# A hybrid SSD and S5 encoder block on one core: masks by affine selects on POOL, rows by one DMA from ACT's queue, a recurrence of three operations a step

## The chip, the cores and the metric

The kernel runs on one core of a Trainium2 chip. The metric is the device time of one execution in microseconds (us). Before the change three runs took 2913.18, 2923.3 and 2929.7 us; their median, 2923.3 us, is the time before. The engines are PE (TensorE, matrix products), DVE (VectorE), ACT (ScalarE), POOL (GpSimd) and SP (SyncE, which here only issues DMAs). Each engine works through its own queue of instructions in order; a wait at the head of a queue holds everything behind it.

## The reference, cut to what matters

One layer of an encoder for 2048 tokens of width 1024, float32 throughout. Beside projections and a feed-forward part it has two mixers, and the change lies in these two.

```
# SSD, per direction, per chunk of 128 tokens; 16 heads in 4 groups, state 128
a_cs  = cumsum(dt * a)                                   # along the chunk
seg   = exp(where(tril, a_cs[q] - a_cs[s], -inf))        # 128 x 128 per head
y     = (C B^T * seg) @ (x * dt)  +  C @ prev * exp(a_cs)
state = B^T @ (x * dt * exp(a_cs[end] - a_cs))           # one per chunk, then a scan over chunks
# S5, per direction: 32 groups of 16 channels, 64 complex states each
h[t] = A * h[t-1] + B u[t]                               # complex, diagonal A
y[t] = Re(C h[t])
```

The backward direction is the same with time reversed: its mask is the upper triangle.

## The kernel before, in words

The program has three large parts in time. Up to about 330 us the input is normalised and the S5 tables are made. From about 330 to 1170 us the SSD mixer and the S5 recurrence and outputs run. From there on come the output projection and the feed-forward part, which the change doesn't touch.

The SSD mixer works in two rounds: first the second half of the sequence (half = 1, chunks 15 down to 8), then the first half (half = 0, chunks 7 down to 0). In a round, `group` handles one of four head groups: `conv_tile` four times (matrix products of the projection on PE, copies out of PSUM on ACT, four multiply-adds at L692 and a gate at L695 on DVE), and then eight calls of `ssd_unit`, one per chunk. So a round has 32 units; this text numbers them 0 to 31 in the order worked.

A unit loads `rw`, the cumulated decays of 4 heads for both directions, copied to all 128 partitions (two DMAs of 256 KB from SP, L747), and `eb` (L751). It adds the mask `msk` (0 or -1e30) to both halves of `rw` (L753): on DVE in the first round (chunk 8 and above), on POOL in the second. ACT takes eight exponentials (L764) into `Lt`. DVE adds the two directions (L766) and multiplies by the scores (L767); PE multiplies by x (L770) and by the state (L776). DVE weights x for the chunk's own state, once for each direction (L790); PE makes that state (L791); ACT copies the forward one out (L795) and SP stores it (L796). `rw` and `Lt` have two buffers each, so the rows of a unit can be loaded once the exponentials of the unit two before it are done.

The S5 recurrence (`recur`, L336 to L350) walks over 126 steps of 128 x 64 numbers on POOL, four operations a step: two products with `s5ar` and `s5ai`, their sum, and the addition to `s5V`. Each step needs the one before. Then POOL issues 16 DMAs that store the states (`store_states`, L356), which the S5 outputs of the second round read.

The order of the instructions on each engine is fixed when the program is built, by a scheduler that simulates it with estimated times (`schedule_with_timeline_sim`). The recurrence's steps get priorities that spread them over the groups of the first round (L350's caller, RS = 0.9).

Of the kernel before, what the change touches and what calls it, by code (L numbers as in the profile page):

```python
# [17 lines left out]
P = 128  # L18
# [17 lines left out]
def bcast(ap, axis, n):  # L36
    a = [list(d) for d in ap.ap]
    a.insert(axis, [0, n])
    return bass.AP(ap.tensor, ap.offset, a)
# [63 lines left out]
class S5:  # L103


    def __init__(self, nc, tc, ident, keep, ps, pp, dr, prm, ud, ys_d):
        self.nc, self.tc, self.ident = nc, tc, ident
        self.keep, self.ps, self.pp, self.dr = keep, ps, pp, dr
        self.prm, self.ud, self.ys_d = prm, ud, ys_d
        self.od = dr.tile([NG5, 2, 2, 64, 256], F32, name="s5od")  # L110
        self.xd = dr.tile([NK5, P, 1024], F32, name="s5xd")
        self.vd = dr.tile([NG5, 2, 2, 64, P], F32, name="s5vd")
        self.td = dr.tile([16, NG5, 31, 16], F32, name="s5td")
        self.ar = keep.tile([P, 2, 32], F32, name="s5ar")
        self.ai = keep.tile([P, 2, 32], F32, name="s5ai")
        self.gb = keep.tile([P, 2, NG5], F32, name="s5gb")
# [4 lines left out]
    def params(self, cst, sp):  # L121
# [48 lines left out]
        for d in range(2):  # L170
            rows = slice(64 * d, 64 * d + 64)
            for g in range(2):
                src = pw[64 * g:64 * g + 64, 16, :, 16 * d:16 * d + 16]
                dr_ = self.ar[rows].rearrange("p r (k g) -> p r k g", g=2)[:, :, :, g]
                di_ = self.ai[rows].rearrange("p r (k g) -> p r k g", g=2)[:, :, :, g]
                v.tensor_copy(dr_, bcast(src[:, 0], 1, 2))
                v.tensor_scalar(di_[:, 0], src[:, 1], -1.0, None, ALU.mult)
                v.tensor_copy(di_[:, 1], src[:, 1])
        den = sp.tile(sh, F32, name="s5den")
# [156 lines left out]
    def recur(self, vp, at_step):  # L336
        nc = self.nc
        V = self.V[:, :, :, :]
        t0 = vp.tile([P, 2, NG5], F32, name="s5r0")
        t1 = vp.tile([P, 2, NG5], F32, name="s5r1")  # L340
        rs = NG5 * P
        at = lambda j: view(V, j, [[rs, 2], [P, NG5]])
        sw = lambda j: view(V, rs + j, [[-rs, 2], [P, NG5]])
        v = nc.gpsimd
        for j in range(1, P - 1):
            with at_step(j):
                v.tensor_tensor(t0, at(j - 1), self.ar, ALU.mult)
                v.tensor_tensor(t1, sw(j - 1), self.ai, ALU.mult)
                v.tensor_tensor(t0, t0, t1, ALU.add)
                v.tensor_tensor(at(j), at(j), t0, ALU.add)  # L350

# [65 lines left out]
class Block:  # L417
# [308 lines left out]

    def masks(self, cst):
        nc = self.nc
        self.msk = cst.tile([P, 2, P], F32, name="msk")
        nc.gpsimd.memset(self.msk, 0.0)  # L730
        nc.gpsimd.affine_select(self.msk[:, 0], self.msk[:, 0], pattern=[[1, P]], compare_op=ALU.is_ge,
                                fill=-1e30, base=0, channel_multiplier=-1)
        nc.gpsimd.affine_select(self.msk[:, 1], self.msk[:, 1], pattern=[[-1, P]], compare_op=ALU.is_ge,
                                fill=-1e30, base=0, channel_multiplier=1)


    def rows_bc(self, src_d, ch, r0, n):
        s = src_d[ch, r0:r0 + n, :]
        return s.rearrange("r t -> (r t)").partition_broadcast(P)

    def ssd_unit(self, sp, pp, g, ch, sl):
# [3 lines left out]
        rw = sp.tile([P, 2, 4, P], F32, name="rw", bufs=2)  # L745
        for d in range(2):
            nc.sync.dma_start(rw[:, d].rearrange("p h q -> p (h q)"), self.rows_bc(self.acs_d, ch, 16 * d + 4 * g, 4))  # L747
        eb = sp.tile([P, 2, P], F32, name="eb", bufs=2)
# [3 lines left out]
        for d in range(2):  # L752
            (v if ch >= 8 else nc.gpsimd).tensor_tensor(rw[:, d], rw[:, d], bcast(self.msk[:, d], 1, 4), ALU.add)  # L753
        pt = pp.tile([P, 512], F32, name="ptb", tag="tb", bufs=2)
# [29 lines left out]
        xw = sp.tile([P, 2, 4, 64], F32, name="xw", bufs=2)  # L784
        st = pp.tile([P, 512], F32, name="pst", tag="st", bufs=1)
        for d in range(2):
            if (d == 0 and ch == 15) or (d == 1 and ch == 0):
                continue
            wv = bcast(self.tok[:, 1, ch % 4, ch // 4, 16 * d + 4 * g:16 * d + 4 * g + 4], 2, 64)
            v.tensor_tensor(xw[:, d], xb[:, 0:256].rearrange("p (h q) -> p h q", h=4), wv, ALU.mult)  # L790
            nc.tensor.matmul(st[:, 256 * d:256 * d + 256], xb[:, 256:384], xw[:, d].rearrange("p h q -> p (h q)"),  # L791
                             start=True, stop=True)
            if d == 0:
                sf = sp.tile([P, 256], F32, name="sf", bufs=2)
                nc.scalar.copy(sf, st[:, 0:256])  # L795
                nc.sync.dma_start(self.sf_d[ch][:, g], sf)  # L796
            elif ch == 15:
# [400 lines left out]
def hybrid_block_kernel(ctx: ExitStack, tc: tile.TileContext, *aps):  # L1198
# [9 lines left out]
    with ExitStack() as mix:  # L1208
# [46 lines left out]
        with pool(name="s5v", bufs=1) as vp, ExitStack() as xs:  # L1255
# [8 lines left out]
            xp = xs.enter_context(pool(name="s5xa", bufs=1))  # L1264
            b.masks(late)
            b.sb = late.tile([P, 4, 256], F32, name="sb")
# [104 lines left out]
```

## Time and profile before

| | |
|---|---|
| median of three runs | 2923.3 us |
| the profiled execution, device time | 2930.28 us |
| its span in the trace | 2928.5 us |
| PE busy | 2701.5 us (92%) |
| DVE busy | 2197.4 us (75%) |
| ACT busy | 1364.4 us (47%) |
| POOL busy | 653.9 us (22%) |

The profile is of one execution. A line of a view names an engine, a line of the kernel, the operation and the tiles (written <- read), with the shape; "idle before" is how long the engine stood still ahead of it, and the name behind the arrow is what ended the wait. Shares over the whole span hide that the engines' load differs by stage, so the rows below are cut by stretches: the first round of units lies in about 329 to 718 us, the second in about 718 to 1170 us.

### The profile page before, as it was taken

The page shows a single profiled execution, that of the slowest core. Times are in us where ns is not written, and L with a number is a line of the kernel's source. Part 1 is how long each engine was busy: PE and PEld are TensorE (multiplying, and loading weights), DVE is VectorE, ACT ScalarE, POOL GpSimd, SP SyncE. Part 2 cuts the span into 40 slices and gives each one's busy share as a digit, 9 for nine tenths or more (in the row PEclk, how much of TensorE's full clock was granted, in tenths as well). Part 3 has the DMA queues.
Part 4 walks back from the last instruction along what each step waited for, and adds up shares of the span by engine and source line. Part 5 has one row for each costly group of instructions (what it writes and reads, how often), then busy time and mean ns, then how long its engine had stood idle before and what let it go on. Part 6 is the DMA issues. An engine that isn't in the chain of part 4 may idle for free.

```text
span 2928.5 us, 37294 instructions
## 1 busy us (share of the span) xinstructions
PE 2701.5 (92%) x12952; PEld 2181.7 (74%) x12952; DVE 2197.4 (75%) x3255; ACT 1364.4 (47%) x2329; POOL 653.9 (22%) x1133
## 2 busy tenths in 40 slices
PE   6998899876999998899898999999999999999997
PEld 4666899765877886677776878787877777877776
DVE  5997688786786776677767777779887888656587
ACT  4542455444567665334235444446444445333254
POOL 0443499992233332111120000000000000000012
PEclk9999999988999999999998999999999999999999
DMA  4546633448455656957845234325444337456464
GB/s 129 173 133 198 168 114 121 112 128 227 134 175 162 188 163 204 252 170 201 252 141 187 79 108 137 107 77 193 149 136 130 121 131 243 160 204 194 150 233 158
DMA packets 507400, 471.55 MB, mean 161 GB/s; under 512 B 90364, under 2 KB 417356, under 8 KB 507212
## 3 DMA queue, kind: packets, MB, share of 16 engines
q1 hardware_dynamic: 504972, 463.99, 52.4%
q0 software_dynamic: 2240, 5.18, 0.7%
q8 instruction: 102, 1.67, 0.2%
q14 instruction: 86, 0.70, 0.1%
HBM read 324.37 MB, written 144.67 MB: 160 GB/s over the span
## 4 chain that ended last, share of the span: by engine, by line
PE 40%; DMA 8%; DVE 7%; issue 2%; ACT 2%; POOL 1%; SPq 0%; ACTq 0%; DVEq 0%; POOLq 0%
PE pA L1040 17%; PE pB L1040 9%; PE pD L1040 5%; PE p L444 3%; PE p L445 2%; PE p L446 2%; DMA ar<-act_d 2%; DVE ll L440 1%; DMA bs<-in_ffn_w_down_dram 1%; DMA wr<-in_ffn_w_up_dram 1%; DMA bs<-hop_d 1%; DMA wt_d<-bs 1%; PE po L846 1%; DVE tl L1027 1%; DMA tst<-in_ffn_w_down_dram 0%
## 5 line engine op out<-in xcount | busy, mean ns | idle before, releaser
L1040 PE MATMUL pA<-th,lh 128*128 128x512 f32 x1056 | 423.7, 402 | 28.3 <-ACT pc L1088 18.8
L1040 PE MATMUL pA<-tl,lh 128*128 128x512 f32 x1056 | 422.1, 400 | 4.2 <-DVE tl L1027 4.2
L1040 PE MATMUL pA<-th,ll 128*128 128x512 f32 x1056 | 420.5, 399 | 0.8 <-DVE ll L440 0.8
L444 PE MATMUL pmm<-hh,wh 128*128 128x512 f32 (+1 forms) x896 | 333.9, 373 | 3.7 <-DVE zt L706 2.4
L445 PE MATMUL pmm<-hl,wh 128*128 128x512 f32 (+1 forms) x896 | 332.7, 371 | 0.0
L446 PE MATMUL pmm<-hh,wl 128*128 128x512 f32 (+1 forms) x896 | 330.2, 369 | 0.0
L1040 PEld LDWEIGHTS pA<-th,lh 128*128 128x128 f32 x1056 | 200.6, 190 | 86.7 <-ACT pc L1088 27.4
L1040 PEld LDWEIGHTS pA<-tl,lh 128*128 128x128 f32 x1056 | 200.7, 190 | 54.2 <-DVE tl L1027 6.4
L1040 PEld LDWEIGHTS pA<-th,ll 128*128 128x128 f32 x1056 | 200.6, 190 | 50.3 <-DVE ll L440 1.6
L1040 PE MATMUL pB<-tl,lh 128*128 128x512 f32 x528 | 209.6, 397 | 1.8 <-DVE tl L1027 1.8
L1040 PE MATMUL pB<-th,lh 128*128 128x512 f32 x528 | 209.7, 397 | 1.8 <-ACT lh L439 1.6
L1040 PE MATMUL pB<-th,ll 128*128 128x512 f32 x528 | 209.2, 397 | 0.0
L1088 ACT COPY pc<-pA 128x512 f32<-128x512 f32 x204 | 116.0, 584 | 185.4 <-PE pA L1040 184.4
L444 PEld LDWEIGHTS pmm<-hh,wh 128*128 128x128 f32 x896 | 169.9, 190 | 30.2 <-issue 3.7
L445 PEld LDWEIGHTS pmm<-hl,wh 128*128 128x128 f32 x896 | 169.8, 190 | 22.6 <-issue 2.5
L764 ACT ACTIVATE Lt<-rw,tokS 128x128 f32<-128x128 f32 x512 | 157.4, 389 | 61.3 <-PE pyd L770 48.7
L446 PEld LDWEIGHTS pmm<-hh,wl 128*128 128x128 f32 x896 | 169.6, 189 | 21.3 <-issue 1.1
L692 DVE SCALAR_TENSOR_TENSOR xbc<-rb,cw,xbc 128x1024 f32<-128x1024 f32 x128 | 178.7, 1399 | 3.8 <-ACT xbc L690 2.8
L444 PE MATMUL p<-wo,yh 128*128 128x512 f32 x384 | 157.3, 410 | 22.2 <-ACT yh L439 21.3
L439 ACT CAST lh<-s 128x512 fp32r<-128x512 f32 (+3 forms) x136 | 109.1, 815 | 123.8 <-DVE s L1007 71.2
L440 DVE TENSOR_TENSOR ll<-s,lh 128x1024 fp32r<-128x1024 f32 (+3 forms) x136 | 126.3, 933 | 52.5 <-PE pA L1040 43.7
L445 PE MATMUL p<-wo,yh 128*128 128x512 f32 x384 | 155.6, 405 | 0.0
(421 smaller groups left out, 6139.0 us busy)
## 6 DMA issues: line engine op xcount, KB each, us to landing
wr<-in_ffn_w_up_dram SPq DMA_DIRECT2D x88, 512.0 KB
rw<-acs_d SPq DMA_DIRECT2D x128, 256.0 KB
wraw<-in_w_in_dram SPq DMA_DIRECT2D x52, 512.0 KB
ar<-act_d SPq DMA_DIRECT2D x32, 512.0 KB
yp_d<-cv SPq DMA_DIRECT2D x32, 512.0 KB
cv<-yp_d SPq DMA_DIRECT2D x32, 512.0 KB
tst<-hop_d SPq DMA_DIRECT2D x28, 512.0 KB
act_d<-cv SPq DMA_DIRECT2D x22, 512.5 KB
```

The source lines that it names most:

```text
L439: self.nc.scalar.copy(hi, src)
L440: self.nc.vector.tensor_tensor(lo, src, hi.bitcast(F32), ALU.subtract)
L444: mm(ps, lhs[0], rhs[0], start=first, stop=False)
L445: mm(ps, lhs[0], rhs[1], start=False, stop=False)
L446: mm(ps, lhs[1], rhs[0], start=False, stop=last)
L692: nc.vector.scalar_tensor_tensor(ac, rb[:, j:j + 1024], cw(j), ac, ALU.mult, ALU.add)
L764: nc.scalar.activation(Lt[:, d, h], rw[:, d, h], AF.Exp, bias=tk(0, d, h))
L846: nc.tensor.matmul(po[:, 2 * (g - 2 * q) + j], self.fst[:, g, 128 * j:128 * j + 128], ct[:, g], start=True, stop=True)
L1027: nc.vector.tensor_tensor(l, st[:, 0:n], h.bitcast(F32), ALU.subtract)
L1040: mm(ps, x, y, start=first and k == i == 0, stop=k == kt - 1 and i == 2, skip_group_check=not first)
L1088: self.nc.scalar.copy(t, src)
```

## The change

Four edits. In a unit, the mask is no longer added from a tile: two affine selects on POOL (L739 of the changed kernel) write -1e30 where the triangle excludes an element, in both rounds. The two loads of `rw` become one DMA of 512 KB, issued from ACT's queue (L731), and the store of the forward state is issued from ACT's queue as well (L784). The two weightings of x become one operation over both directions. In the recurrence a step has one product of 128 x 128 numbers, with the coefficients laid out as a 2 x 2 block (`s5aq`, L345), and two additions of 128 x 64 into `s5V` (L347). The diff:

```diff
@@ -111,8 +111,7 @@
         self.xd = dr.tile([NK5, P, 1024], F32, name="s5xd")
         self.vd = dr.tile([NG5, 2, 2, 64, P], F32, name="s5vd")
         self.td = dr.tile([16, NG5, 31, 16], F32, name="s5td")
-        self.ar = keep.tile([P, 2, 32], F32, name="s5ar")
-        self.ai = keep.tile([P, 2, 32], F32, name="s5ai")
+        self.aq = keep.tile([P, 2, 2, 32], F32, name="s5aq")
         self.gb = keep.tile([P, 2, NG5], F32, name="s5gb")
 
     def pst(self, name):
@@ -171,11 +170,11 @@
             rows = slice(64 * d, 64 * d + 64)
             for g in range(2):
                 src = pw[64 * g:64 * g + 64, 16, :, 16 * d:16 * d + 16]
-                dr_ = self.ar[rows].rearrange("p r (k g) -> p r k g", g=2)[:, :, :, g]
-                di_ = self.ai[rows].rearrange("p r (k g) -> p r k g", g=2)[:, :, :, g]
-                v.tensor_copy(dr_, bcast(src[:, 0], 1, 2))
-                v.tensor_scalar(di_[:, 0], src[:, 1], -1.0, None, ALU.mult)
-                v.tensor_copy(di_[:, 1], src[:, 1])
+                aq = lambda o, r: self.aq[rows, o, r].rearrange("p (k g) -> p k g", g=2)[:, :, g]
+                for o in range(2):
+                    v.tensor_copy(aq(o, o), src[:, 0])
+                v.tensor_scalar(aq(0, 1), src[:, 1], -1.0, None, ALU.mult)
+                v.tensor_copy(aq(1, 0), src[:, 1])
         den = sp.tile(sh, F32, name="s5den")
         u0 = sp.tile(sh, F32, name="s5u0")
         u1 = sp.tile(sh, F32, name="s5u1")
@@ -336,18 +335,16 @@
     def recur(self, vp, at_step):
         nc = self.nc
         V = self.V[:, :, :, :]
-        t0 = vp.tile([P, 2, NG5], F32, name="s5r0")
-        t1 = vp.tile([P, 2, NG5], F32, name="s5r1")
+        t = vp.tile([P, 2, 2, NG5], F32, name="s5r0")
         rs = NG5 * P
         at = lambda j: view(V, j, [[rs, 2], [P, NG5]])
-        sw = lambda j: view(V, rs + j, [[-rs, 2], [P, NG5]])
+        both = lambda j: view(V, j, [[0, 2], [rs, 2], [P, NG5]])
         v = nc.gpsimd
         for j in range(1, P - 1):
             with at_step(j):
-                v.tensor_tensor(t0, at(j - 1), self.ar, ALU.mult)
-                v.tensor_tensor(t1, sw(j - 1), self.ai, ALU.mult)
-                v.tensor_tensor(t0, t0, t1, ALU.add)
-                v.tensor_tensor(at(j), at(j), t0, ALU.add)
+                v.tensor_tensor(t, both(j - 1), self.aq, ALU.mult)
+                for r in range(2):
+                    v.tensor_tensor(at(j), at(j), t[:, :, r], ALU.add)
 
     def store_states(self):
         for r in range(2):
@@ -724,33 +721,23 @@
         for g in range(2):
             nc.sync.dma_start(self.dsk[64 * g:64 * g + 64], dsrc[g].partition_broadcast(64))
 
-    def masks(self, cst):
-        nc = self.nc
-        self.msk = cst.tile([P, 2, P], F32, name="msk")
-        nc.gpsimd.memset(self.msk, 0.0)
-        nc.gpsimd.affine_select(self.msk[:, 0], self.msk[:, 0], pattern=[[1, P]], compare_op=ALU.is_ge,
-                                fill=-1e30, base=0, channel_multiplier=-1)
-        nc.gpsimd.affine_select(self.msk[:, 1], self.msk[:, 1], pattern=[[-1, P]], compare_op=ALU.is_ge,
-                                fill=-1e30, base=0, channel_multiplier=1)
-
-
-    def rows_bc(self, src_d, ch, r0, n):
-        s = src_d[ch, r0:r0 + n, :]
-        return s.rearrange("r t -> (r t)").partition_broadcast(P)
 
     def ssd_unit(self, sp, pp, g, ch, sl):
         nc = self.nc
         v = nc.vector
         Bt, Ct, x0, x1 = (t[:, 128 * (ch % 8):128 * (ch % 8) + 128] for t in sl)
         rw = sp.tile([P, 2, 4, P], F32, name="rw", bufs=2)
-        for d in range(2):
-            nc.sync.dma_start(rw[:, d].rearrange("p h q -> p (h q)"), self.rows_bc(self.acs_d, ch, 16 * d + 4 * g, 4))
+        acs = self.acs_d[:, :, :]
+        nc.scalar.dma_start(rw.rearrange("p d h q -> p d (h q)"),
+                            bass.AP(acs.tensor, acs.offset + P * (32 * ch + 4 * g), [[0, P], [16 * P, 2], [1, 512]]))
         eb = sp.tile([P, 2, P], F32, name="eb", bufs=2)
         es = self.eac_d[ch, 16 + 4 * g:16 + 4 * g + 4, :].rearrange("(j g) t -> g j t", g=2)
         for gg in range(2):
             nc.sync.dma_start(eb[64 * gg:64 * gg + 64], es[gg].partition_broadcast(64))
         for d in range(2):
-            (v if ch >= 8 else nc.gpsimd).tensor_tensor(rw[:, d], rw[:, d], bcast(self.msk[:, d], 1, 4), ALU.add)
+            o = -1 if d else 1
+            nc.gpsimd.affine_select(rw[:, d], rw[:, d], pattern=[[0, 4], [o, P]], compare_op=ALU.is_ge,
+                                    fill=-1e30, base=0, channel_multiplier=-o)
         pt = pp.tile([P, 512], F32, name="ptb", tag="tb", bufs=2)
         for j, t in enumerate((x0, x1, Bt)):
             nc.tensor.transpose(pt[:, 128 * j:128 * j + 128], t, self.ident)
@@ -783,17 +770,18 @@
         nc.sync.dma_start(self.y_d[ch][:, 2 * g:2 * g + 2, :], y)
         xw = sp.tile([P, 2, 4, 64], F32, name="xw", bufs=2)
         st = pp.tile([P, 512], F32, name="pst", tag="st", bufs=1)
+        tok = self.tok[:, :, :, :, :]
+        v.tensor_tensor(xw, view(xb[:, :], 0, [[0, 2], [64, 4], [1, 64]]),
+                        view(tok, 512 + 128 * (ch % 4) + 32 * (ch // 4) + 4 * g, [[16, 2], [1, 4], [0, 64]]), ALU.mult)
         for d in range(2):
             if (d == 0 and ch == 15) or (d == 1 and ch == 0):
                 continue
-            wv = bcast(self.tok[:, 1, ch % 4, ch // 4, 16 * d + 4 * g:16 * d + 4 * g + 4], 2, 64)
-            v.tensor_tensor(xw[:, d], xb[:, 0:256].rearrange("p (h q) -> p h q", h=4), wv, ALU.mult)
             nc.tensor.matmul(st[:, 256 * d:256 * d + 256], xb[:, 256:384], xw[:, d].rearrange("p h q -> p (h q)"),
                              start=True, stop=True)
             if d == 0:
                 sf = sp.tile([P, 256], F32, name="sf", bufs=2)
                 nc.scalar.copy(sf, st[:, 0:256])
-                nc.sync.dma_start(self.sf_d[ch][:, g], sf)
+                nc.scalar.dma_start(self.sf_d[ch][:, g], sf)
             elif ch == 15:
                 nc.scalar.copy(self.sb[:, g], st[:, 256:512])
             else:
@@ -1262,7 +1250,6 @@
                     s5.inputs(vp, wk)
             sp = rs.enter_context(right("sp"))
             xp = xs.enter_context(pool(name="s5xa", bufs=1))
-            b.masks(late)
             b.sb = late.tile([P, 4, 256], F32, name="sb")
             p0 = tc.cur_priority
             for g in range(GA):
```

How this moves instructions is seen on two engines. On POOL, a place inside the recurrence. L347 to L350 are the four operations of a step before:

```order
L347 TENSOR_TENSOR s5r_6272<-s5V,s5ar 128x64
L348 TENSOR_TENSOR s5r_6273<-s5V,s5ai 128x64
L349 TENSOR_TENSOR s5r_6272<-s5r_6272,s5r_6273 128x64
L350 TENSOR_TENSOR s5V<-s5V,s5r_6272 128x64
L347 TENSOR_TENSOR s5r_6272<-s5V,s5ar 128x64
```

In the changed kernel L345 is the product and L347 the additions of a step, and L739 are the selects; these are the rows at steps 39 to 43:

```order
L345 TENSOR_TENSOR s5r_6335<-s5V,s5aq 128x128
L347 TENSOR_TENSOR s5V<-s5V,s5r_6335 128x64 x2
L345 TENSOR_TENSOR s5r_6335<-s5V,s5aq 128x128
L347 TENSOR_TENSOR s5V<-s5V,s5r_6335 128x64 x2
L739 AFFINE_SELECT rw<-rw 128x512 x2
L345 TENSOR_TENSOR s5r_6335<-s5V,s5aq 128x128
L347 TENSOR_TENSOR s5V<-s5V,s5r_6335 128x64 x2
L345 TENSOR_TENSOR s5r_6335<-s5V,s5aq 128x128
L347 TENSOR_TENSOR s5V<-s5V,s5r_6335 128x64 x2
L345 TENSOR_TENSOR s5r_6335<-s5V,s5aq 128x128
L739 AFFINE_SELECT rw<-rw 128x512 x2
L347 TENSOR_TENSOR s5V<-s5V,s5r_6335 128x64 x2
```

A step is three instructions, and pairs of selects stand between the steps; the first pair here is that of unit 4, the second that of unit 5. In the whole queue the pairs of units 0 to 3 stand behind steps 2 to 7, those of units 4 to 11 behind steps 40 to 75, that of unit 12 behind step 92, and that of unit 19 inside step 125.

On POOL again, the end of the recurrence before, where L356 are the 16 stores of the states, L397 belongs to the S5 outputs and L753 to the units of the second round:

```order
L349 TENSOR_TENSOR s5r_6272<-s5r_6272,s5r_6273 128x64
L350 TENSOR_TENSOR s5V<-s5V,s5r_6272 128x64
L356 DMA s5vd<-s5V 64x8x128 x16
L397 TENSOR_TENSOR s5bd<-s5gw,s5bm 128x128 x4
L753 TENSOR_TENSOR rw<-rw,msk 128x512 x8
```

and in the changed kernel, where L353 are the stores:

```order
L739 AFFINE_SELECT rw<-rw 128x512 x2
L347 TENSOR_TENSOR s5V<-s5V,s5r_6335 128x64
L345 TENSOR_TENSOR s5r_6335<-s5V,s5aq 128x128
L347 TENSOR_TENSOR s5V<-s5V,s5r_6335 128x64 x2
L353 DMA s5vd<-s5V 64x8x128 x16
L739 AFFINE_SELECT rw<-rw 128x512 x26
L394 TENSOR_TENSOR s5bd<-s5gw,s5bm 128x128 x4
```

Of the 64 selects of the first round 40 (units 0 to 19) stand ahead of the stores, and 24 (units 20 to 31) behind them, with two of the second round.

On ACT, two units of the first round before, where L764 are the exponentials, L795 is the copy of the forward state and SP issues the DMAs:

```order
L759 COPY xb<-ptb 128x384
L764 ACTIVATE Lt<-rw,tokS 128x128 x8
L439 CAST wh<-wraw 128x1024
L679 COPY rb<-pmm 128x342
L795 COPY sf<-pst 128x256
```

and in the changed kernel, where L751 are the exponentials, L731 is the load of the rows of the unit two further on, L783 the copy and L784 its store:

```order
L746 COPY xb<-ptb 128x384
L751 ACTIVATE Lt<-rw,tokS 128x128 x8
L676 COPY rb<-pmm 128x342
L731 DMA rw<-acs_d 128x2x512
L783 COPY sf<-pst 128x256
L784 DMA sf_d<-sf 128x256
```

The load now stands in ACT's queue close behind the exponentials that free its buffer, and ACT issues it itself.

## Rows read from the trace of the kernel before

**Rows 1.** Windows, all engines: two of the first round, one of the second.

```profile
core 0: us, PE busy (x) PEld busy (x) DVE busy (x) ACT busy (x) POOL busy (x), PEclk, DMA share, GB/s
329.00:594.00 265.00, 249.31 (x1569) 229.94 (x1568) 222.63 (x336) 134.43 (x301) 241.80 (x391) 0.97 0.41 117
594.00:718.00 124.00, 85.12 (x456) 67.13 (x455) 94.41 (x174) 58.55 (x144) 76.37 (x136) 0.79 0.64 174
718.00:1150.00 432.00, 419.23 (x2278) 345.17 (x2277) 326.18 (x517) 270.71 (x527) 124.24 (x116) 0.99 0.59 167
```

**Rows 2.** Waits of PE at 329 to 718 us: us, times, longest.

```profile
PE ptb L756 <- DVE xbc L695: 11.4, 2, 10.8
```

**Rows 3.** Groups of DVE at 329 to 594 us: busy us, mean ns.

```profile
L692 DVE SCALAR_TENSOR_TENSOR xbc<-rb,cw,xbc 128x1024 f32<-128x1024 f32 x55 | 73.5, 1343 | 0.8 <-ACT xbc L690 0.4
L753 DVE TENSOR_TENSOR rw<-rw,msk 128x512 f32<-128x512 f32 x44 | 33.5, 767 | 23.9 <-DMA rw<-acs_d 23.9
...
L801 DVE TENSOR_TENSOR sb<-sb,decb 128x256 f32<-128x256 f32 x15 | 6.8, 453 | 0.0
```

**Rows 4.** Timeline of POOL: one step of the recurrence and the next's start.

```profile
608.35 0.35 POOL L347 TENSOR_TENSOR s5r<-s5V,s5ar 128x64 f32<-128x64 f32 x1
...
609.08 0.32 POOL L349 TENSOR_TENSOR s5r<-s5r,s5r 128x64 f32<-128x64 f32 x1
609.47 0.37 POOL L350 TENSOR_TENSOR s5V<-s5V,s5r 128x64 f32<-128x64 f32 x1
609.92 0.36 POOL L347 TENSOR_TENSOR s5r<-s5V,s5ar 128x64 f32<-128x64 f32 x1
```

**Rows 5.** Timelines of POOL and DVE at 621 to 624 us.

```profile
621.37 1.40 POOL L348 TENSOR_TENSOR s5r<-s5V,s5ai 128x64 f32<-128x64 f32 x1
622.84 1.21 POOL L349 TENSOR_TENSOR s5r<-s5r,s5r 128x64 f32<-128x64 f32 x1
...
621.28 2.59 DVE L692 SCALAR_TENSOR_TENSOR xbc<-rb,cw,xbc 128x1024 f32<-128x1024 f32 x2
```

**Rows 6.** Instructions on the tile s5bd: duration ns min/median/max.

```profile
L397 POOL TENSOR_TENSOR s5bd<-s5gw,s5bm x64: 394/424/1392, 710.5 to 1170.3; 128x128 f32<-128x128 f32 x64
```

**Rows 7.** Groups of POOL over the span.

```profile
L753 POOL TENSOR_TENSOR rw<-rw,msk 128x512 f32<-128x512 f32 x64 | 97.0, 1527 | 232.0 <-DMA rw<-acs_d 213.6 <-ACT s5gt L394 14.7 <-ACT xb L759 3.6
...
L733 POOL TENSOR_SCALAR_AFFINE_SELECT msk<-msk 128x128 f32<-128x128 f32 x1 | 0.7, 734 | 0.0
L614 POOL MEMSET dtz<- 128x512 f32 x1 | 0.6, 578 | 0.0
...
L731 POOL TENSOR_SCALAR_AFFINE_SELECT msk<-msk 128x128 f32<-128x128 f32 x1 | 0.3, 292 | 0.1
```

**Rows 8.** Timeline of POOL: first and last of the rows of the 16 stores.

```profile
662.12 0.74 POOL L356 DMA_DIRECT2D s5vd<-s5V  x1 [0.29 <-POOL s5V L350]
...
677.42 0.69 POOL L356 DMA_DIRECT2D s5vd<-s5V  x1 [0.28 <-DMA s5vd<-s5V]
```

**Rows 9.** Timeline of DVE: unit 20's second mask and product; the first round's last product.

```profile
583.75 0.74 DVE L753 TENSOR_TENSOR rw<-rw,msk 128x512 f32<-128x512 f32 x1 [0.43 <-DMA rw<-acs_d]
...
602.64 0.68 DVE L767 TENSOR_TENSOR Lt<-Lt,ptb 128x512 f32<-128x512 f32 x1
...
723.35 0.68 DVE L767 TENSOR_TENSOR Lt<-Lt,ptb 128x512 f32<-128x512 f32 x1
```

**Rows 10.** Group of the exponentials on the page; SP's loads on the tile rw.

```profile
L764 ACT ACTIVATE Lt<-rw,tokS 128x128 f32<-128x128 f32 x512 | 157.4, 389 | 61.3 <-PE pyd L770 48.7 <-DVE rw L753 7.3 <-DMA eb<-eac_d 1.7
...
L747 SPq DMA_DIRECT2D rw<-acs_d x128: 319/424/2771, 327.5 to 1127.4; - x128
```

**Rows 11.** DVE at 594 to 718 us: its longest wait, and the masks' group.

```profile
DVE rw L753 <- DMA rw<-acs_d: 22.4, 6, 9.2
...
L753 DVE TENSOR_TENSOR rw<-rw,msk 128x512 f32<-128x512 f32 x20 | 15.1, 758 | 22.5 <-DMA rw<-acs_d 22.4
```

**Rows 12.** Waits of POOL at 718 to 1150 us.

```profile
POOL rw L753 <- DMA rw<-acs_d: 211.0, 35, 23.9
```

## The prediction

> **What bounds the kernel now.** I read the windows by stage first. In the second round PE is busy 419.2 of 432 us: it is the bound there, and nothing off PE can be worth more than the 13 us that are left. The first round has room: PE stands idle 15.7 us of the first 265, and 38.9 of the next 124, with a granted clock of 0.79 of its full speed [rows 1]. In those 265 us three engines are nearly full: PE 249.3, POOL 241.8, DVE 222.6. The waits say who holds PE up: the largest is for DVE's conv work, 11.4 us in two waits [rows 2]. From 594 us on DVE itself stands still for the rows of a unit, 22.4 us in six waits [rows 11]. POOL is full, but in the kernel before it does nothing in this round that a unit waits for: its queue holds the recurrence alone, and the unit's masks are DVE's. So POOL's load costs nothing yet. The change makes it count, so I read POOL's timeline next.
>
> **The recurrence.** A step that nothing disturbs takes 1.57 us from start to start (608.35 to 609.92), with operations of 0.32 to 0.37 us and a gap of 0.07 to 0.08 behind one whose result is needed [rows 4]. The new step has one product of 128 numbers and two additions that each need what went before. The product is priced by the operation of this shape on POOL, 0.39 us at its shortest [rows 6], plus 0.03 for each 64 numbers read with a step (0.35 for L347 beside 0.32 for L349, rows 4): 0.45. With two additions at 0.36 and three gaps of 0.08 a step is 1.41 us, and 126 steps are 178 us, where 1.57 makes 198. The product costs no less than 0.39 and no more than the two that it replaces, 0.70: the 178 may be 170 to 209.
>
> The strided reads cost 0.03 us for 64 numbers here [rows 4]. [...]
>
> **The selects.** A select of 128 x 128 took 0.29 us, another, with DVE at work, 0.73; none of 128 x 512 was run. Below stands the memset of that shape, 0.58 us, which reads nothing; above stands the addition of two operands that is replaced, 1.53 us on the mean [rows 7]. I take 0.75, since the select reads one operand and is nearer to the memset.
>
> **What POOL is held up by.** POOL's 391 instructions of the first window took 241.8 us [rows 1]; at the undisturbed 0.35 they would take 137. The 105 us between are collisions with DVE: two L692 of DVE ran from 621.28 to 623.87, and the two operations of POOL that fell into them took 1.40 and 1.21 us [rows 5]. DVE's operations that read two operands from SBUF are eight groups in that window, from 73.5 us (L692) to 6.8 us (L801), 198.6 us together [rows 3]. So POOL loses 0.53 us for each us of such work. Without the masks, 33.5 us of it [rows 3], 165 us remain up to the same place in the work, and POOL loses 87.
>
> **The sum.** Units now wait for POOL in its order. Ahead of the masks of unit 20 its queue holds the whole recurrence (178), 42 selects with that unit's own (31.5), the 16 stores, 662.1 to 678.1 us before, so 16 [rows 8], and the 87 of collisions: 312 us. From 329 us on that is 641 us. Before, unit 20's second mask ended at 584.5 us [rows 9]: the masks are 57 us late there. Not all of that reaches PE: the product that needs the mask ran at 602.64 [rows 9], 18 us later, and eight exponentials at 0.39 [rows 10] and one addition need about 5 with their handovers, my estimate. So 13 us are slack, and unit 20 is 44 us late. Behind the masks that wait on POOL stand, in their own queues, ACT's exponentials and with them the copies out of PSUM, DVE's products with the conv work, and PE's projections: all of it moves with the unit.
>
> What is given back lies behind unit 20, where POOL has only selects to do. DVE loses its 15.1 us of masks, and up to 22.4 us of waits for rows [rows 11], since ACT's queue now loads them right behind the exponentials and the states are stored before. That is 15 to 37.5 us; I take the middle, 26. The round ends 18 us later than before: 44 - 26.
>
> **The rest.** Two DMAs a unit go from SP to ACT. At SP's median of 0.42 us an issue [rows 10] that is 27 us of ACT in a round, beside 193 busy us of 389 in the first and 271 of 432 in the second [rows 1]: free time hides it. Uncovered it would cost those 27 us, and one issue took 2.77. In the second round the select is shorter than the addition, but POOL sits 211 us there waiting for rows [rows 12], and PE is full: nothing, at most 13 us gained. One weighting of x instead of two saves DVE a start in each unit and moves no wait: nothing. The coefficients are four small copies either way.
>
> So the profiled execution, 2930.3 us, becomes 2948. The median of the runs lies 7.0 us below it: 2941 us.
>
> **The rivals.**
>
> *The relief wins (faster).* If POOL keeps pace, the masks that leave DVE (33.5 and 15.1 us) and the 22.4 us of waits go from a round whose PE is idle for 54.6 us. That idle time is the most there is; half to two thirds of it is 30 us, so 2893. For it speak PE's longest wait and DVE's load; against it the 312 us. It decides where unit 20's masks come by 597 us (584.5 and 13 of slack), in 268 us from the start: 225.5 us of it are steps, selects and stores, so collisions would have to cost 42 instead of 87 us, 0.26 us for each us of DVE's work. They may: three larger operations a step can be caught less often than four.
>
> *Nothing is given back (slower by more).* Behind unit 20 the units form a chain: select, exponentials, load of the rows two units on, select. Today DVE loses 22.4 us to those loads and SP issues them ahead. If each costs as much again, only the 15 us of masks come back and the select is dear at 1.2 us: 44 + 19 - 15 = 48; with the waits of POOL for late rows inside the recurrence, some 12 more, 60: 2983.
>
> *It cancels.* Collisions at 0.4 (66 us instead of 87) and all 37.5 given back: 44 - 21 - 37.5, about -15 at the extreme, and around zero in the middle: 2923.
>
> **How the numbers follow.** I give the forecast 0.45 with a range of its own from 2928 to 2958, the relief 0.22, nothing given back 0.20, cancelling 0.13. With all bounds at their low ends unit 20 isn't late and the relief stands, -45; with selects and product at their high ends and 15 given back it would be +93, which needs every bound at once. So the range runs from 2888 to 2988 us. Half a per cent, 14.6 us, is what a measurement can tell from no change: faster means under 2909, slower over 2938. The relief is faster (0.22); three fifths of the forecast and the rival in which nothing is given back are slower (0.27 + 0.20); the rest is the same (0.31).
>
> **What would show it.** In the profile after: a mean of POOL's product near 0.45 us undisturbed and of selects near 0.75; collisions of about 0.5 us for each us of DVE's two-operand work; unit 20's selects at about 640 us, behind the stores; ACT idle ahead of its exponentials with POOL as the releaser; PE's idle time in the first round spread over its first 265 us. The forecast is wrong if unit 20's selects end before about 600 us, if ACT waits for the loads and not for POOL, or if a stage other than the first round changes by over 10 us.

## The result and the profile after

The changed kernel takes 2969.62 us in the median of four runs (2965.37 to 2973.24), the kernel before, beside it, 2925.41 us (four runs). The ratio is 1.0157 with a 95% interval of 1.0122 to 1.0193: slower by 1.6%. The profiled execution took 2965.37 us with a span of 2963.6 us, 35.1 us more than before; the profiled execution before lies above all four of its runs, the one after is the fastest of its four, so the profiles show less than the 44 us between the medians.

The windows of the changed kernel, with the columns of [rows 1]:

```profile
329.00:594.00 265.00, 212.47 (x1278) 194.22 (x1277) 162.78 (x222) 108.33 (x241) 237.06 (x366) 0.91 0.35 95
594.00:718.00 124.00, 94.79 (x558) 81.67 (x558) 84.44 (x132) 57.67 (x134) 63.80 (x85) 0.85 0.55 151
718.00:1150.00 432.00, 418.56 (x2280) 344.37 (x2276) 300.12 (x504) 264.95 (x536) 82.66 (x120) 0.99 0.63 173
```

The loss lies in the first window. PE does 212 us of work there instead of 249, DVE 163 instead of 223, and ACT 108 instead of 134; only POOL is as full as before. In the second window PE works off 10 us more than before, in the third the same. Who waits for whom, at 329 to 765 us (engine and line, releaser: us, times, longest), is plain:

```profile
ACT Lt L751 <- POOL rw L739: 103.7, 14, 24.2
DVE Lt L753 <- ACT Lt L751: 91.7, 16, 23.5
POOL rw L739 <- DMA rw<-acs_d: 62.1, 9, 15.2
...
PE pmm L441 <- ACT rb L676: 50.4, 6, 20.3
```

This is one chain. POOL is late with the selects, ACT's exponentials stand at the head of ACT's queue until then, DVE's sum waits for the exponentials, and the copies of PE's products out of PSUM (L676) stand behind the exponentials on ACT, so PE waits too. Before, ACT and PE had no wait for POOL in this round; PE's largest there was 11.4 us in two waits [rows 2].

The first long wait of ACT for POOL (before it the longest was 4.2 us) is that of unit 4. POOL's timeline of the changed kernel around it:

```profile
423.70 0.51 POOL L345 TENSOR_TENSOR s5r<-s5V,s5aq 128x128 f32<-128x128 f32 x1
424.29 0.80 POOL L347 TENSOR_TENSOR s5V<-s5V,s5r 128x64 f32<-128x64 f32 x2
425.04 1.22 POOL L739 TENSOR_SCALAR_AFFINE_SELECT rw<-rw 128x512 f32<-128x512 f32 x2
426.22 0.51 POOL L345 TENSOR_TENSOR s5r<-s5V,s5aq 128x128 f32<-128x128 f32 x1
```

and ACT's, where the brackets give the idle time and its releaser:

```profile
394.56 0.37 ACTq L731 DMA_DIRECT2D rw<-acs_d  x1
...
425.70 2.44 ACT L751 ACTIVATE Lt<-rw,tokS 128x128 f32<-128x128 f32 x8 [22.54 <-POOL rw L739]
```

PE waited 18.6 us for the copies that stood behind these exponentials; its granted clock, 1.00 at 400 to 412 us, was 0.50 at 420 to 430, and 1.00 again from 434. What such stretches add to the loss wasn't separated from the waits. POOL waited for nobody there (26.9 us busy of the 31 from 395 to 426 us): 33 steps of the recurrence, which nobody needs before the second round, stood ahead of unit 4's selects. Unit 4's product, at 413 us before, comes at 433. Unit 12's comes 48 us late (557, 509 before) and unit 20's and unit 31's as follows, beside 602.64 and 723.35 in [rows 9]:

```profile
662.48 0.68 DVE L754 TENSOR_TENSOR Lt<-Lt,ptb 128x512 f32<-128x512 f32 x1
...
765.19 0.68 DVE L754 TENSOR_TENSOR Lt<-Lt,ptb 128x512 f32<-128x512 f32 x1
```

Unit 20 is 60 us late, unit 31 42, the first unit of the second round 36 (810 instead of 774), its last 42 (1196.6 instead of 1154.2). POOL's groups at 329 to 657.5 us, where unit 20's selects end, carry the terms of the forecast's sum (busy us, mean ns, idle before):

```profile
L347 POOL TENSOR_TENSOR s5V<-s5V,s5r 128x64 f32<-128x64 f32 x252 | 152.7, 606 | 18.3
L345 POOL TENSOR_TENSOR s5r<-s5V,s5aq 128x128 f32<-128x128 f32 x126 | 92.9, 738 | 33.0 <-DVE s5V L333 23.5
L739 POOL TENSOR_SCALAR_AFFINE_SELECT rw<-rw 128x512 f32<-128x512 f32 x43 | 35.0, 835 | 2.5 <-DMA eb<-eac_d 1.9 <-DMA rw<-acs_d 0.6
L353 POOL DMA_DIRECT2D s5vd<-s5V x16 | 11.0, 693 | 7.8 <-DMA s5vd<-s5V 7.0 <-issue 0.4 <-POOL s5V L347 0.3
```

The step without a neighbour at work, to be held against [rows 4], takes 1.47 us from start to start (532.14 to 533.61):

```profile
532.14 0.51 POOL L345 TENSOR_TENSOR s5r<-s5V,s5aq 128x128 f32<-128x128 f32 x1
532.73 0.80 POOL L347 TENSOR_TENSOR s5V<-s5V,s5r 128x64 f32<-128x64 f32 x2
533.61 0.51 POOL L345 TENSOR_TENSOR s5r<-s5V,s5aq 128x128 f32<-128x128 f32 x1
```

### The profile page after: what moved, and what is told of

Read it like the earlier page. It is cut to its first block, busy times and chain, and to the rows that moved or that the text cites. A ratio compares the mean times of both kernels' runs of the same rounds, so it can differ in the third digit from the quotient of the medians.

```text
span 2963.6 us, 37150 instructions
## 1 busy us (share of the span) xinstructions
PE 2703.7 (91%) x12952; PEld 2187.8 (74%) x12952; DVE 2126.1 (72%) x3139; ACT 1360.7 (46%) x2325; POOL 602.2 (20%) x1068
## 4 chain that ended last, share of the span: by engine, by line
PE 62%; DMA 12%; POOL 9%; DVE 8%; issue 4%; ACT 3%; SPq 1%; ACTq 0%; DVEq 0%; POOLq 0%
PE pA L1028 19%; PE pB L1028 10%; PE pD L1028 5%; POOL s5V L347 5%; PE pmm L441 3%; PE pmm L442 3%; PE pmm L443 3%; POOL s5r L345 3%; PE p L441 3%; PE p L442 3%; PE p L443 3%; DMA ar<-act_d 2%; PE s5py L383 2%; PE pst L779 1%; POOL rw L739 1%
## 5 line engine op out<-in xcount | busy, mean ns | idle before, releaser
L1028 PEld LDWEIGHTS pA<-tl,lh 128*128 128x128 f32 x1056 | 200.3, 190 | 54.5 <-DVE tl L1015 6.7
L751 ACT ACTIVATE Lt<-rw,tokS 128x128 f32<-128x128 f32 x512 | 157.3, 389 | 129.9 <-POOL rw L739 103.7
L442 PEld LDWEIGHTS pmm<-hl,wh 128*128 128x128 f32 x896 | 171.7, 192 | 22.5 <-issue 2.1
L441 PE MATMUL p<-wo,yh 128*128 128x512 f32 x384 | 157.8, 411 | 21.3 <-ACT yh L436 20.3
L689 DVE SCALAR_TENSOR_TENSOR xbc<-rb,cw,xbc 128x1024 f32<-128x1024 f32 x128 | 171.4, 1339 | 6.1 <-ACT xbc L687 5.0
L739 POOL TENSOR_SCALAR_AFFINE_SELECT rw<-rw 128x512 f32<-128x512 f32 x128 | 104.1, 836 | 348.2 <-DMA rw<-acs_d 306.6
```

The lines of the kernel that those rows point to most:

```text
L441: mm(ps, lhs[0], rhs[0], start=first, stop=False)
L442: mm(ps, lhs[0], rhs[1], start=False, stop=False)
L689: nc.vector.scalar_tensor_tensor(ac, rb[:, j:j + 1024], cw(j), ac, ALU.mult, ALU.add)
L739: nc.gpsimd.affine_select(rw[:, d], rw[:, d], pattern=[[0, 4], [o, P]], compare_op=ALU.is_ge, fill=-1e30, base=0, channel_multiplier=-o)
L751: nc.scalar.activation(Lt[:, d, h], rw[:, d, h], AF.Exp, bias=tk(0, d, h))
L1028: mm(ps, x, y, start=first and k == i == 0, stop=k == kt - 1 and i == 2, skip_group_check=not first)
```

## The experiments

Twelve kernels ran, four on a chip at a time, 4 to 12 runs of each, with the kernel before beside them. Ratios are to the kernel before on the same chip. The products in the last column are those of one profiled execution, whose time differs from the kernel's median by up to 10 us. From the last unit of the second round on, these executions took another 1767 to 1781 us, in no order that follows the change, so a few us at a unit need not reach the end.

| kernel | median, us | ratio | 95% interval | product of unit 12, 20, 31 at |
|---|---|---|---|---|
| before (profile) | 2925.4 | 1 | | 509, 603, 723 |
| whole change (profile after) | 2969.6 | 1.0157 | 1.0122 to 1.0193 | 557, 662, 765 |
| whole, first round's masks on DVE | 2937.3 | 1.0029 | 1.0013 to 1.0046 | 518, 612, 725 |
| selects alone | 2959.4 | 1.0105 | 1.0088 to 1.0122 | 550, 667, 759 |
| recurrence alone | 2943.9 | 1.0041 | 1.0025 to 1.0058 | 516, 615, 732 |
| DMAs from ACT alone | 2942.8 | 1.0045 | 1.0028 to 1.0062 | 515, 612, 733 |
| whole, 63 steps | 2929.4 | 0.9994 | 0.9981 to 1.0006 | 540, 624, 727 |
| whole, stores from SP | 2987.3 | 1.0193 | 1.0175 to 1.0212 | 555, 678, 780 |
| whole, 4 steps a unit | 2921.1 | 0.9972 | 0.9960 to 0.9985 | 510, 600, 712 |
| selects, one weighting, 4 steps a unit | 2921.4 | 0.9972 | 0.9960 to 0.9984 | 507, 599, 707 |
| the same, 5 steps a unit | 2940.9 | 1.0036 | 1.0019 to 1.0053 | 517, 620, 739 |
| the same, 6 steps a unit | 2960.7 | 1.0108 | 1.0085 to 1.0131 | 534, 644, 761 |
| whole, 5 steps a unit | 2952.2 | 1.0077 | 1.0054 to 1.0099 | 518, 617, 737 |
| 5 steps a unit, three operations, SP's DMAs | 2944.9 | 1.0051 | 1.0030 to 1.0072 | 514, 613, 729 |

### One part undone, one part alone

The whole change with the first round's masks given back to DVE:

```diff
-            nc.gpsimd.affine_select(rw[:, d], rw[:, d], pattern=[[0, 4], [o, P]], compare_op=ALU.is_ge,
-                                    fill=-1e30, base=0, channel_multiplier=-o)
+            if ch >= 8:
+                v.tensor_tensor(rw[:, d], rw[:, d], bcast(self.msk[:, d], 1, 4), ALU.add)
+            else:
+                nc.gpsimd.affine_select(rw[:, d], rw[:, d], pattern=[[0, 4], [o, P]], compare_op=ALU.is_ge,
+                                        fill=-1e30, base=0, channel_multiplier=-o)
```

> The changed kernel with one thing undone: in the first round DVE adds the mask tile again; selects in the second round, the DMAs from ACT, the three-operation recurrence and the one weighting stay. Theory (the first round goes at the pace of POOL's queue, where masks stand among the recurrence): the loss goes, 2925 us within 10, a ratio to before of 0.995 to 1.003. Rival A (the loads and stores from ACT's queue come late or hold ACT up): stays near 2965, ratio 1.013. Rival B (the new order of the whole program, whichever engine masks): stays above 2945, ratio over 1.007.

1.0029, just inside the theory's range of ratios: four fifths of the loss go with 64 masks. What is left, 0.3%, isn't that of the first round's selects. The kernel before with nothing but the selects, in both rounds:

```diff
-            (v if ch >= 8 else nc.gpsimd).tensor_tensor(rw[:, d], rw[:, d], bcast(self.msk[:, d], 1, 4), ALU.add)
+            o = -1 if d else 1
+            nc.gpsimd.affine_select(rw[:, d], rw[:, d], pattern=[[0, 4], [o, P]], compare_op=ALU.is_ge,
+                                    fill=-1e30, base=0, channel_multiplier=-o)
```

> The kernel before with one part of the change alone: all masks by affine selects on POOL; four operations a step, DMAs from SP, two weightings stay. Theory: the whole loss and a little more, since a step undisturbed takes 1.57 instead of 1.47 us (12 us over 126 steps): 2970 to 2990 us, ratio 1.015 to 1.022. Rival A: 2925 us, ratio within 0.005 of 1. Rival B: anything between, since the order changes too; then POOL is not the releaser of ACT's exponentials in the first round.

1.0105, under the range of the theory, but with the same wait of ACT (at 329 to 765 us):

```profile
ACT Lt L756 <- POOL rw L744: 104.6, 12, 23.4
```

The selects alone make two thirds of the loss. Two other parts alone, first the recurrence:

```diff
-                v.tensor_tensor(t0, at(j - 1), self.ar, ALU.mult)
-                v.tensor_tensor(t1, sw(j - 1), self.ai, ALU.mult)
-                v.tensor_tensor(t0, t0, t1, ALU.add)
-                v.tensor_tensor(at(j), at(j), t0, ALU.add)
+                v.tensor_tensor(t, both(j - 1), self.aq, ALU.mult)
+                for r in range(2):
+                    v.tensor_tensor(at(j), at(j), t[:, :, r], ALU.add)
```

> The kernel before with the three-operation recurrence alone. Theory: nothing in the first round waits for the recurrence while the masks are DVE's, so 2925 us within 8; the recurrence ends about 10 to 25 us earlier than the 661.8 us of before. Rival (the longer product blocks DVE more than the shorter operations did): slower by 10 us or more.

and then the DMAs:

```diff
-        for d in range(2):
-            nc.sync.dma_start(rw[:, d].rearrange("p h q -> p (h q)"), self.rows_bc(...))
+        nc.scalar.dma_start(rw.rearrange("p d h q -> p d (h q)"), bass.AP(...))
...
-                nc.sync.dma_start(self.sf_d[ch][:, g], sf)
+                nc.scalar.dma_start(self.sf_d[ch][:, g], sf)
```

> The kernel before with the rows by one DMA from ACT's queue and the forward states stored from there, alone. Theory: ACT has free time for the issues: 2925 us within 8, perhaps 5 to 15 less because the 22 us of DVE's waits for rows at 594 to 718 us shrink. Rival A: 2950 to 2970 us, with waits for the rows grown in the first round.

Both cost, 0.41% and 0.45%. The forecast put ACT's issues at nothing and didn't count what the product costs DVE. For the recurrence that is the time of its rival, 16 us over the kernel before beside it; for the issues it is neither account's. The three parts alone sum to 1.9%, more than the whole; the single weighting wasn't run alone. The recurrence of three operations ends 35 us earlier (626.9 instead of 661.8), but DVE's operations become longer. Two groups of DVE at 345 to 626 us, before:

```profile
L440 DVE TENSOR_TENSOR wl<-wraw,wh 128x1024 fp32r<-128x1024 f32 x17 | 22.2, 1306 | 1.5 <-ACT wh L439 1.4
L790 DVE TENSOR_TENSOR xw<-xb,tokS 128x256 f32<-128x256 f32 x43 | 20.2, 506 | 0.0
```

and with the new recurrence alone:

```profile
L437 DVE TENSOR_TENSOR wl<-wraw,wh 128x1024 fp32r<-128x1024 f32 x17 | 23.7, 1393 | 3.5 <-ACT wh L436 3.5
L787 DVE TENSOR_TENSOR xw<-xb,tokS 128x256 f32<-128x256 f32 x40 | 21.1, 563 | 0.0
```

The same work is 7% and 11% longer. Over DVE's eight groups that read two operands from SBUF, the longer means make some 11 us up to 626 us, an estimate from such rows, and unit 20's product is 12 us late (615, 603). In this kernel DVE still adds the masks and is among the engines that hold PE up [rows 2], so it fits the loss; that it is all of it wasn't tested, and the profiled execution, 2934.0 us, is 10 us under the median. Why the issues from ACT cost 0.45% stays open: units were already some 8 us late at unit 0, and I found no single new wait in the trace that is as large. The sign of its rival is absent: DVE's waits for the rows fell at 329 to 718 us, from 46.3 to 30.7 us.

### Less in the queue

The whole change with 63 of the 126 steps:

```diff
-        for j in range(1, P - 1):
-            with at_step(j):
+        for j in range(1, P // 2):
+            with at_step(2 * j):
```

> The changed kernel with only the first 63 of the 126 steps of the recurrence: the other 63 are left out, so its S5 states are not those of the reference. Theory (units wait for POOL because the whole recurrence stands ahead of unit 20's selects): 63 steps at 1.47 us, about 93 us, and some 40 us of collisions go from POOL's queue; unit 20's product comes at or before its time before the change (602.6 us) instead of 662.5, the waits of ACT for selects fall from 104 us to under 40, and the time is 2880 to 2915 us, under that of before. Rival (the loads and the units' own chain select, exponentials, load hold the units up, not the recurrence): unit 20 stays later than 625 us and the time stays over 2940.

2929 us: the loss goes, but no gain comes, and unit 20's product is at 624 us; neither account had that. The trace says why. The halved recurrence wasn't spread further: steps 8 to 40 stood ahead of unit 4's selects, as in the whole change. ACT's waits at 395 to 445 us:

```profile
ACT Lt L751 <- POOL rw L739: 22.6, 1, 22.6
```

As long as in the whole change, where the wait was 22.5 us. Unit 12 is 31 us late. The recurrence is through at 485 us, and behind it the units catch up: unit 31 is only 4 us late. So the load counts too, since half of it takes the loss away; but what stands ahead of a unit delays it whatever the total, and over the round ACT still waited 54.5 us for POOL, where under 40 were expected.

The 16 stores issued from SP:

```diff
-                    self.nc.gpsimd.dma_start(self.vd[g:g + 8, d, r]...
+                    self.nc.sync.dma_start(self.vd[g:g + 8, d, r]...
```

> The changed kernel with the 16 stores of the states issued from SP's queue instead of POOL's. Theory (what stands ahead of unit 20's selects on POOL delays them one for one): the 18.6 us of issues go from POOL's queue, unit 20's selects come at about 640 instead of 656 us, and since 24 units' selects wait behind them the time falls by 10 to 18 us, to 2951 to 2960. Rival (the units behind unit 20 are bound by the loads of their rows, which catch up whatever unit 20 does): unit 20 is earlier, but unit 31's product stays at about 765 us and the time within 5 us of 2970. A third way: SP, which waits for the states, holds loads behind the stores, and the time rises.

The time didn't fall to the 2951 to 2960 us of the theory: it is 2987 us, 1.0193 of before. The interval overlaps that of the whole change, so the times alone don't settle a rise; in the trace unit 31 is 15 us later than in the whole change (780, 765). That is the third way. SP's timeline:

```profile
604.31 0.33 SPq L770 DMA_DIRECT2D y_d<-yy  x1
634.07 4.81 SPq L353 DMA_DIRECT2D s5vd<-s5V  x5
638.98 1.20 SPq L657 DMA_DIRECT2D wraw<-in_w_in_dram  x1
640.22 13.48 SPq L353 DMA_DIRECT2D s5vd<-s5V  x11
653.80 1.38 SPq L516 DMA_DIRECT2D wraw<-in_x_dram  x1
```

SP waited with the first store for the recurrence, from 604.6 to 634, and everything behind it waited too. ACT needed the input behind the stores (L516):

```profile
659.74 1.15 ACT L521 ACTIVATE wraw<-wraw,rs 128x1024 f32<-128x1024 f32 x1 [33.38 <-DMA wraw<-in_x_dram]
```

### The same work in another order

The whole change, with steps held to the units: POOL writes one number behind a unit's selects, and step 4k overwrites its buffer from it, so it can't stand ahead of unit k.

```diff
+            tk_ = self.ticks.tile([1, 4], F32, name="tick", bufs=32)
+            nc.gpsimd.tensor_copy(tk_[:, 0:1], rw[0:1, 1, 0, 0:1])
...
+                if j % 4 == 0 and j // 4 < 32:
+                    v.tensor_copy(t[0:1, 0, 0, 0:1], self.ticked[j // 4][:, 0:1])
                 v.tensor_tensor(t, both(j - 1), self.aq, ALU.mult)
```

> The changed kernel with one tiny copy on POOL behind each unit's selects, which step 4k of the recurrence overwrites for unit k: the order keeps four steps to a unit over all 32 units, instead of the 126 steps within the first 20. Theory (the order on POOL is the cause): no unit's selects wait for more than some steps; unit 20's product at about 605 instead of 662 us, unit 31's at 715 to 730 instead of 765, the time 2905 to 2935 us, though the stores come later. Rival (POOL is too slow in any order: 126 steps, 64 selects, stores and collisions make some 340 us of 390): units are late evenly, unit 31's product at over 745, time over 2950. A second rival: the late stores delay the S5 outputs in the second round, unit 31 on time but the second round longer by over 10 us.

Nothing is removed, 63 small copies are added, and the loss is gone: 1.0157 becomes 0.9972. The windows:

```profile
329.00:594.00 265.00, 252.38 (x1567) 233.41 (x1567) 202.54 (x280) 133.49 (x294) 226.33 (x315) 0.97 0.44 117
594.00:718.00 124.00, 95.84 (x518) 75.96 (x517) 93.26 (x154) 68.78 (x167) 111.61 (x205) 0.88 0.60 153
```

and the largest wait of ACT at 329 to 765 us:

```profile
ACT Lt L757 <- POOL rw L741: 48.4, 14, 7.5
```

PE's work in the first window is 252 us again. As many waits for POOL, 14, are left, but the longest is 7.5 instead of 24.2 us. Unit 31 is 11 us earlier than before; the first unit of the second round is 9 us earlier (765, 774), and the whole gains 8. The chain of work that ended last runs at 705 to 734 us through the recurrence's last step and the stores' landing (start, us, what):

```profile
705.63 1.46 POOL s5V L349
707.38 0.74 POOL s5vd L355
708.48 3.42 POOL s5vd L355 x5
711.90 8.15 DMA s5vd<-s5V
...
721.84 11.36 DMA s5vd<-s5V
733.86 0.47 SPq L363
```

The same pace with the old recurrence and SP's DMAs:

```diff
+                if j % 4 == 0 and j // 4 < 32:
+                    v.tensor_copy(t0[0:1, 0, 0:1], self.ticked[j // 4][:, 0:1])
                 v.tensor_tensor(t0, at(j - 1), self.ar, ALU.mult)
```

> The kernel before with the selects on POOL in both rounds, one weighting of x, and the paced order, but with the old recurrence of four operations and the loads and the store issued by SP as before. It leaves out the two parts that cost 0.4% each by themselves. Theory (order is what makes the selects dear, and the issues from ACT and the longer product are costs of their own): 2900 to 2930 us, some 10 to 15 below the paced kernel with the whole change. Rival (a step of 1.57 instead of 1.47 us and its fourth collision cost POOL more than they spare DVE): at or over the paced kernel with the whole change.

2921.36 beside 2921.14 us: the expected 10 to 15 us between them don't exist. At this pace the three operations and ACT's DMAs together neither cost nor gain anything that the intervals can tell (0.12% each way).

Then the same with `j % 5` and `j % 6`, to have the stores earlier:

> The paced kernel with the old recurrence and SP's loads, but step 5k instead of 4k held behind unit k's selects: the recurrence ends with unit 25 and its stores come some 50 us earlier, before the round's end. Theory (in the kernel with four steps to a unit the late stores, 712 to 728 us, and what is read from them give back part of the gain between the rounds: unit 31's product 16 us early, unit 32's 7): unit 31's product at 707 to 715, unit 32's at 758 to 765, time 2905 to 2917 us. Rival (the gap between the rounds is the conv work and weights of the next group, not the stores): no change against four steps, 2917 to 2926 us.

> As the one with five steps to a unit, but six: the recurrence ends with unit 21 or 23, close to the kernel before, and its stores at about 650 to 670 us. Theory: between five steps a unit and the changed kernel's order; units 12 to 22 wait for POOL by some us each, unit 20's product at 605 to 620, time 2912 to 2930 us. Rival (the earlier the stores the better): the fastest of all, under 2910 us.

My theory that the late stores were what is left to win fell, in its sum. The gap between the products of units 31 and 32 did shrink, from 60 to 51 us (before: 51), but unit 31 came 32 us later, in an execution of 2949.8 us, 9 over the median. Five steps took 2941 us and six 2961, over the numbers of theories and rivals alike. ACT's largest wait with five steps, and with six:

```profile
ACT Lt L762 <- POOL rw L746: 83.3, 17, 11.6
```

```profile
ACT Lt L762 <- POOL rw L746: 100.2, 17, 22.0
```

and with four:

```profile
ACT Lt L762 <- POOL rw L746: 62.5, 14, 9.7
```

This is a scale: 4, 5 and 6 steps between two units' selects give 0.9972, 1.0036 and 1.0108. With four POOL is busy 235 and 114 of the round's 389 us, 90%. A unit comes every 12 us (389 in 32). A step is busy 2.2 us here (278 us in 126 steps), a select 0.77 and a small copy 0.47: four steps, two selects and two copies make 11.3 us, five steps 13.5, an estimate by which there is no room for a fifth.

The last two tell the other parts apart at five steps a unit, as diffs to the whole change and to the old recurrence shown above:

> The whole change with five steps of the recurrence held to a unit. Theory: it gains over four steps a unit (0.9972 of before) what the earlier stores give back, some 5 to 10 us, 2910 to 2917 us, and stays some 5 us over the kernel with the old recurrence and SP's loads at the same pace, since the issues from ACT (0.45% by themselves) and the longer product (0.41%) keep costing. Rival (with the order mended these two parts cost nothing, since they cost only through the units' order): within 3 us of that kernel, or below it.

> Selects on POOL, one weighting, the recurrence of three operations, five steps held to a unit, but the loads and the store issued by SP as before: against the whole change at this pace it tells what the issues from ACT cost, against the old recurrence at this pace what the three operations do. Theory (the 128-wide product holds DVE's operations longer, some 9 us over the recurrence, and POOL's shorter steps spare no unit at this pace): 3 to 9 us over the old recurrence, 2915 to 2922 us, and within 5 us of the whole change. Rival (a step shorter by 0.1 us brings the selects earlier): at or below the old recurrence.

The medians stand in the order that the theory had (2941, 2945, 2952 us), but the last two are 23 and 35 us over its ranges, which rested on the gain of the earlier stores. The intervals of neighbours overlap, so each part alone isn't settled at this pace; the two together just are, by 0.4% (1.0077, from 1.0054 on, against 1.0036, up to 1.0053). At four steps a unit the same two cost nothing, so what they cost depends on the order.

## Why the prediction was right

It said slower, by 18 us with a range up to 2988; the runs show 44. The mechanism is the one it named: POOL's queue, in its order, becomes what the units wait for. The size is not: 2969.6 us lies outside the forecast's own range of 2928 to 2958 and nearer to the rival in which nothing is given back (2983). On the profiles the loss is 35 us and not 18. By its own steps:

- *The step.* 1.47 instead of 1.41 us: the product takes 0.51, not 0.45. The forecast put 0.06 for its 128 strided numbers, from 0.35 beside 0.32 us [rows 4], on the 0.39 of the other operation of this shape [rows 6]; measured are 0.12 over that 0.39. How much of the 0.12 the stride makes was not shown.
- *Collisions.* The two groups of the recurrence took 245.6 us and 27.8 of gaps (18.3, and 33.0 less the 23.5 ahead of the first step): 273 us. Less 126 x 1.47 = 185, that is 88 us; the forecast said 87. DVE's groups that read two operands from SBUF took 174 us in that time, so POOL lost 0.50 us for each us of them, as forecast (0.53): that three larger operations are caught much less often (0.26), on which the relief rested, did not happen.
- *Selects and stores.* A select takes 0.637 us undisturbed and 0.835 on the mean here, 35 us for the 31.5; the stores 18.8 for 16. With 2.5 us of waits the sum is 329 instead of 312, and unit 20's selects end at 657.5 instead of 641.
- *Unit 20.* Late by 60 instead of 44, the same 16 us. The slack of 13 was right: selects' end to product is 5.0 us. But the units' delay begins at unit 4, not at unit 20. That the sum holds all the same is in part luck: it adds up POOL's work without asking when each unit needs it, and POOL waited only 2.5 us for loads up to there.
- *What is given back.* 18 us, not 26: this is the term with the wrong reason. The 22.4 us of waits for rows [rows 11] didn't go. They moved to POOL, whose selects waited 62.1 us for `rw`, mostly behind unit 20, since a load is issued only when the late exponentials have run. That is the mechanism of the rival in which nothing is given back; the measured time lies between that rival's and the forecast's. So unit 31 is 42 us late and not 18, 16 us by the sum and 8 by this term. Of the 42, 35 reach the end of the profiled execution; that 7 come back behind the second round was in no account and stays open.
- *The rest.* The second round gave nothing, as said (36 us late at its first unit, 42 at its last), and ACT's issues took 0.37 us. "Free time hides it" does not hold in the kernel before, where the same issues cost 0.45%; with four steps a unit they and the three operations together cost nothing.
- *The relief.* It exists: with POOL in pace unit 31 comes 11 to 16 us earlier than before. Of the 30 us that the rival gave it, 8 reach the end. Part of the lead goes between the rounds, where the stores then come late: at four steps a unit it falls there from 11 to 9 us in the whole change, from 16 to 7 with the old recurrence.

## What to carry to other kernels

Before work that others wait for is moved to an engine whose load nobody waits for, read that engine's queue in order, not its share of the span: what matters is how much unneeded work stands ahead of each needed piece. If the total fits, hold the unneeded work to the pace of the needed; here one dependency for each unit was worth 1.8%, while halving the load without it brought 1.6% and left out half of the result. And a store that waits for a long computation must not stand in a queue that feeds others: here it held SP's queue for 29 us, and unit 31 came 15 us later than with the stores on POOL.

## What the runs showed that I had not expected

The neighbour's cost runs both ways: POOL's operation of 128 x 128 lengthened DVE's `wl` from 1.31 to 1.39 us and `xw` from 0.51 to 0.56 (the recurrence alone), where the prediction counted only what DVE costs POOL. Copies of a single number on POOL took 0.42 to 0.51 us on the mean (29 us for 63 in the paced kernel) beside DVE's work, not much less than an operation on 128 x 64 (0.61 there); the shortest took 0.17.
